# Wider moving operands in a hybrid token-mixer trunk: 512 weight columns past stationary activations

## The chip, the core and the metric

One NeuronCore of a Trainium2 chip. The metric is the device time of one execution in microseconds, the median of several runs.

## The reference, cut to what matters

Two layers over 256 tokens and a model width of 1024, all in float32. `h` is a layer norm, modulated by adaLN; `w_in` has 14248 columns, which go to four token mixers, their gates `z` and the merge gates.

```python
for l in range(2):
    shift, scale, gate = split(silu(c) @ w_ada[l] + b_ada[l], 3)
    h = layernorm(x) * (1 + scale) + shift
    q_a,k_a,v_a, q_b,k_b,v_b,beta,decay, cq,ckv,kpe, qkv_d, z, merge = split(h @ w_in[l])
    o_a = diff_attention(...)        # branch A
    o_b = gated_delta_rule(...)      # branch B: short convolution, scan over 4 chunks of 64 tokens
    o_c = mla(...)                   # branch C
    o_d = dilated_attention(...)     # branch D: 3 dilations, 8 heads
    branches = stack([o_a, o_b, o_c, o_d]) * silu(z)
    merged = einsum('snc,ncd,snd->sd', branches, w_br[l], sigmoid(merge))
    x = layernorm(ALPHA * x + gate * (merged @ w_out[l])) * ln_g[l] + ln_b[l]
```

## The kernel before

**Split products.** A large product is made of three float32r matmuls for each 128 rows of the contraction. Each operand is split into a high part that float32r holds exactly and a low part: `hh` and `hl` for the activations, `wh` and `wl` for the weights. `load_w` (L519) fetches half a unit's weights as a tile of 128 x 1024 (512 KB) into `wr` on SP's DMA queue, ScalarE casts it to `wh` (L466), and VectorE (GpSimd for a few) subtracts to get `wl` (L470, L469). There are four buffers each of `wr`, `wh` and `wl`.

**Units.** `w_in` is cut into units of 256 columns (`UW`). A unit is 48 matmuls of 256 moving columns: 8 tiles of the contraction, 3 products, and 2 tiles of its output. Two forms exist:

- `token_proj` / `token_mm` (L546, L556), for the first four units, A and D: 128 tokens of `h^T` are stationary, 256 weight columns move. Both token tiles of a unit share one PSUM bank. For each of the two token tiles all eight contraction tiles are gone through.
- `feat_proj` (L564), for B, the gates `z`, the merge gates and the branch products (24 matmuls there): 128 weight columns are stationary, 256 tokens move, and features come out on the partitions.

The output projection (`do_out`, L1342) uses `token_mm` on `mh` and `ml`, the merged values with features on partitions.

**PSUM.** Eight banks: three for these products ("mm"), two for branch B, two for scores, one for transposes. Queries and keys of A and D go through `rotated_transpose` (L576): ScalarE copies the unit (L581), VectorE rotates part of it (L424 to L427), and the transposes `tu_...` (L588) are kept back until the matmuls of one more unit are issued (`deferred`, `flush`).

**The order of work.** `layer_items` makes a list of items, one for each unit and each quarter of a branch product: first units, B (6), rest of A (4), then the phases of the branches C, A, B, D in that order. A phase is 2 gate units, and 4 times a merge unit and a quarter of the branch product. Half of D's units stands between the phases of C and A, the other half between A and B. Weights are fetched two items ahead (`AHEAD`). The mixers are generators; after each item `step_streams` moves each running one on by a rate (`RATE`: B, A, D 1.0; C 2.0; adaLN of the next layer 0.7 steps). A phase's first gate unit (`do_z`, u = 0) first runs what is left of its branch at once (`finish`). The order on each engine is then made by a list scheduler from this program order and its own simulated times.

**Written orders.** In the first layer the adaLN sums are made from loaded weights, and the first units are multiplied by quarters of the contraction as `h^T` comes; four matmuls with a zero operand open their banks, and `start_order` (L438) fixes the order on the engines. Before the second layer, `in_order` puts the power of the layer norm (`pow`, on GpSimd) between the subtractions of weight pieces.

Of the kernel before, what the change touches and what calls it, by code (L numbers as in the profile page):

```python
# [15 lines left out]
ALU = mybir.AluOpType  # L16
# [16 lines left out]
UW = 256  # L33
SLABS = {"b": 20, "q": 14, "c": 4, "d": 6, "tk": 2, "hf": 4, "p": 8, "o": 6}
# [3 lines left out]
HT1 = 3  # L38
# [6 lines left out]
START_VECTOR = ((0, 0), (1, 0), (1, 1), (3, 1))  # L45


def _unit_columns():
    """Column ranges of w_in in units of up to 256, and whether a unit's weights are stationary."""
    units, where = [], {}  # L50

    def add(name, start, n, feat):
        where[name] = len(units)
        for u in range(0, n, UW):
            units.append((start + u, min(UW, n - u), feat))
# [9 lines left out]
    return units, where  # L65


UNITS, WHERE = _unit_columns()
# [71 lines left out]
def _layout(a):  # L140
# [10 lines left out]
    wi = np.zeros((L, len(UNITS), 2, P, 1024), f32)  # L151
    for u, (c0, n, feat) in enumerate(UNITS):
        cols = np.zeros((L, 8, P, UW), f32)
        cols[..., :n] = w_in[..., c0:c0 + n]
        if u == WHERE["ckv"]:
            cols[..., n:n + 8] = w_in[..., OFF["beta"]:OFF["beta"] + 8]
        if feat:
            wi[:, u] = cols.reshape(L, 8, P, 2, P).transpose(0, 3, 2, 1, 4).reshape(L, 2, P, 1024)
        else:
            wi[:, u] = cols.reshape(L, 2, 4, P, UW).transpose(0, 1, 3, 2, 4).reshape(L, 2, P, 1024)  # L160
    out["win"] = wi
    w = a["w_br"].reshape(L, 4, 4, P, 4, UW)
    out["wbr"] = np.ascontiguousarray(w.transpose(0, 1, 4, 3, 2, 5)).reshape(L, 4, 4, P, 1024)
    w = a["w_out"].reshape(L, 2, 4, P, 4, UW)
    out["wout"] = np.ascontiguousarray(w.transpose(0, 4, 1, 3, 2, 5)).reshape(L, 4, 2, P, 1024)
# [31 lines left out]
def kernel(ctx: ExitStack, tc: tile.TileContext, d, out, dbg=None, nlayers=DEPTH):  # L197
# [34 lines left out]
    # ------------------------------------------------------------ first loads  # L232
# [31 lines left out]
    zero = cpool.tile([P, P], BF16, name="zero")  # L264
    G.memset(zero, 0.0)
# [10 lines left out]
    # ------------------------------------------------------------ silu(c), adaLN  # L276
# [69 lines left out]
    # ------------------------------------------------------------ constants of the mixers  # L346
# [70 lines left out]
    # ------------------------------------------------------------ helpers  # L417
    def rope(dst, src, nh, n, name):
        """dst, src: [P, 2, nh, 2 * n]; src may be in PSUM."""
        cc, ss = rt[n]  # L420
        tmp = s2.tile([P, 2, nh, 2 * n], F32, tag="ropet", name=f"ropet_{name}")
        ccb = cc.rearrange("p t a n -> p t (a n)").unsqueeze(2).to_broadcast([P, 2, nh, 2 * n])
        ssb = ss.rearrange("p t a n -> p t (a n)").unsqueeze(2).to_broadcast([P, 2, nh, 2 * n])
        V.tensor_tensor(tmp[:, :, :, 0:n], src[:, :, :, n:2 * n], ssb[:, :, :, 0:n], ALU.mult)  # L424
        V.tensor_tensor(tmp[:, :, :, n:2 * n], src[:, :, :, 0:n], ssb[:, :, :, n:2 * n], ALU.mult)
# [11 lines left out]

    def start_order():  # L438
        """The order of issue in the first layer's first units, engine by engine."""
        m = marks  # L440
        in_order(m["his00"], m["mod00"], m["h00"], m["his10"], m["his20"], m["his30"])
        in_order(m["acc0"][7], m["los00"], m["hl00"], m["los10"])
        in_order(m["acc2"][4], m["hl01"], m["acc2"][5])
        in_order(m["acc3"][7], m["hl03"])
        in_order(m["q0"][35], m["sum01"], m["q0"][36])
        in_order(m["q1"][23], m["sum02"], m["q1"][24])
# [18 lines left out]
    def split(hi, lo, src, eng=V):  # L465
        marks["hi"] = A.copy(hi, src)  # L466
        if eng is G:
            parts = (tuple(v[:, j:j + 512] for v in (lo, src, hi)) for j in range(0, src.shape[-1], 512))
# [3 lines left out]
    def softmax(dst, ssum, sc, mask, name):  # L472
        """dst = exp(sc + mask - max) and its row sums; sc in PSUM, dst in SBUF."""
# [5 lines left out]
    def pair_scores(lhs, rhs, t, tag, name, nb):  # L479
        """exp of causally masked scores of two maps [P, 2, n], unnormalised, and reciprocal sums [P, 2]."""  # L480
# [15 lines left out]
    def causal_transpose(prs, m, tag, name):  # L496
        """P^T of one map as [P keys, 3, P]: (keys 0, queries 0), (0, 1), (1, 1)."""
# [7 lines left out]
    # ------------------------------------------------------------ projections  # L505
    deferred = []

    def flush():
        """Emits what waits for the matrix products of one more unit."""
        while deferred:  # L510
            deferred.pop(0)()
# [7 lines left out]
    def load_w(src, name, place=None, eng=V):  # L519
        """Half a unit's weights; a function giving columns of the parts that float32r holds exactly."""  # L520
        w = wraw.tile([P, 1024], F32, tag="wr", name=f"wr{name}")
        nc.sync.dma_start(w, src)
# [4 lines left out]
        else:  # L527
            width = 512
# [3 lines left out]
        for j, (a, b) in enumerate(zip(hi, lo)):  # L532
            marks[f"lo{name}"] += split(a, b, w[:, j * width:(j + 1) * width], eng)
            marks[f"hi{name}"].append(marks["hi"])

        def get(c0, n):
            return tuple(a[c0 // width][:, c0 % width:c0 % width + n] for a in (hi, lo))
# [3 lines left out]
    def spare():  # L541
        """Slabs of the attention branches for two more units' weights."""
# [13 lines left out]
    def token_proj(w, hh, hl, name, sel=natural):  # L556
        """[P tokens, 2, 256] in PSUM = h @ w for both token tiles; w: two halves of four d tiles."""
        ps = bank("mm", [P, 2, UW], name)
        for t in range(2):
# [888 lines left out]
```

## Time and profile before

| | us |
|---|---|
| runs: median (lowest to highest of 3) | 1084.03 (1082.26 to 1086.2) |
| span of the profiled execution, first to last instruction | 1080.6 |
| TensorE matmul busy | 1046.7 (97%) |
| TensorE weight load busy | 1003.7 (93%) |
| VectorE busy | 749.0 (69%) |
| ScalarE busy | 557.3 (52%) |
| GpSimd busy | 68.7 (6%) |

The profiled execution has no time of its own beside its span; its 1080.6 us stand 3.4 us below the median of the runs, for what lies around the program's first and last instruction and for the spread of the runs. A matmul's busy time contains the way through the array and overlaps with its neighbours, so the distance between starts, or a count over a stretch, tells the pace, and the mean duration does not.

### The profile page before, as it was taken

To read this page: it belongs to the slowest core of one execution; us is meant where nothing else is said; L and a number is where in the kernel's file an instruction comes from. 1 tells how busy PE (TensorE), PEld (TensorE's weight loads), DVE (VectorE), ACT (ScalarE), POOL (GpSimd) and SP (SyncE) were. 2 spreads that over 40 slices of the span, in tenths; PEclk is the share of its full clock that TensorE was granted. 3 is DMA by queue.
4 is the path that set the end of the run, shared out by engine and by line. 5 is a ranking of instruction groups with operands and counts; after the bars stand their busy time and mean duration, and the time that the engine had idled before them with its cause. 6 is when DMAs were issued, how large, how long until landed. Compare 5 with 4: busy or idle time off the path is not lost. (4 is left out here: it accounts for less than half of the span.)

```text
span 1080.6 us, 21300 instructions
## 1 busy us (share of the span) xinstructions
PE 1046.7 (97%) x8490; PEld 1003.7 (93%) x8490; DVE 749.0 (69%) x1576; ACT 557.3 (52%) x1018; POOL 68.7 (6%) x62
## 2 busy tenths in 40 slices
PE   4799999999999999999989999999999999999997
PEld 3799999999999999999979999899999999999997
DVE  6888778786576664567894886778656555565776
ACT  4376675555454354546535666655455444454550
POOL 2300000010000000000450000001000000000000
PEclk9899999999999999999989999999999999999999
DMA  9963334557554565347762333446644236533551
GB/s 322 326 234 119 118 117 169 182 209 244 169 181 144 192 239 174 118 156 228 228 237 64 135 135 119 160 171 201 194 159 138 98 118 234 178 135 124 199 185 40
DMA packets 67812, 186.24 MB, mean 172 GB/s; under 512 B 13569, under 2 KB 20097, under 8 KB 67713
## 3 DMA queue, kind: packets, MB, share of 16 engines
q1 hardware_dynamic: 67712, 184.88, 49.8%
q8 instruction: 67, 1.10, 0.4%
q14 instruction: 33, 0.26, 0.1%
HBM read 180.39 MB, written 4.46 MB: 171 GB/s over the span
## 5 line engine op out<-in xcount | busy, mean ns | idle before, releaser
L470 DVE TENSOR_TENSOR wl<-wr,wh 128x1024 fp32r<-128x1024 f32 x248 | 303.6, 1226 | 175.2 <-ACT wh L466 174.2
L466 ACT CAST wh<-wr 128x1024 fp32r<-128x1024 f32 x252 | 264.0, 1048 | 279.4 <-PE d L552 99.9
L551 PE MATMUL d<-wh,hh 128*128 128x256 f32 x576 | 166.1, 288 | 0.0
L553 PE MATMUL d<-wl,hh 128*128 128x256 f32 x576 | 163.8, 284 | 0.0
L552 PE MATMUL d<-wh,hl 128*128 128x256 f32 x576 | 163.6, 284 | 0.0
L570 PE MATMUL m<-hh,wh 128*128 128x256 f32 x512 | 148.0, 289 | 0.0
L572 PE MATMUL m<-hh,wl 128*128 128x256 f32 x512 | 146.3, 286 | 0.0
L571 PE MATMUL m<-hl,wh 128*128 128x256 f32 x512 | 145.6, 284 | 0.0
L551 PEld LDWEIGHTS d<-wh,hh 128*128 128x128 f32 x576 | 110.9, 193 | 0.6 <-issue 0.6
L553 PEld LDWEIGHTS d<-wl,hh 128*128 128x128 f32 x576 | 110.8, 192 | 0.5 <-issue 0.5
L552 PEld LDWEIGHTS d<-wh,hl 128*128 128x128 f32 x576 | 110.9, 192 | 0.2 <-issue 0.2
L570 PEld LDWEIGHTS m<-hh,wh 128*128 128x128 f32 x512 | 97.5, 190 | 2.6 <-issue 1.4
L571 PEld LDWEIGHTS m<-hl,wh 128*128 128x128 f32 x512 | 97.6, 191 | 0.8 <-issue 0.6
L572 PEld LDWEIGHTS m<-hh,wl 128*128 128x128 f32 x512 | 97.5, 190 | 0.8 <-issue 0.5
L302 DVE SCALAR_TENSOR_TENSOR ada<-wada,cact,ada 128x512 f32<-128x512 f32 x84 | 68.1, 816 | 20.9 <-DMA wada<-in_wada 19.9
L570 PE MATMUL z<-hh,wh 128*128 128x256 f32 x256 | 73.9, 289 | 0.0
L570 PE MATMUL br<-bh,wh 128*128 128x256 f32 x256 | 73.8, 288 | 0.0
L572 PE MATMUL z<-hh,wl 128*128 128x256 f32 x256 | 72.8, 284 | 0.0
L571 PE MATMUL z<-hl,wh 128*128 128x256 f32 x256 | 72.7, 284 | 0.0
L571 PE MATMUL br<-bl,wh 128*128 128x256 f32 x256 | 72.5, 283 | 0.0
L572 PE MATMUL br<-bh,wl 128*128 128x256 f32 x256 | 72.0, 281 | 0.0
L570 PE MATMUL b<-hh,wh 128*128 128x256 f32 x192 | 56.2, 293 | 0.0
(366 smaller groups left out, 2467.7 us busy)
## 6 DMA issues: line engine op xcount, KB each, us to landing
wr<-in_win SPq DMA_DIRECT2D x212, 512.0 KB
wr<-in_wbr SPq DMA_DIRECT2D x32, 512.0 KB
wada<-in_wada SPq DMA_DIRECT2D x32, 512.0 KB
wada<-in_wada SPq DMA_DIRECT2D x32, 256.0 KB
wrs<-in_win SPq DMA_DIRECT2D x8, 512.0 KB
wro<-in_wout SPq DMA_DIRECT2D x8, 512.0 KB
wr<-in_wout SPq DMA_DIRECT2D x8, 512.0 KB
wrearly<-in_win SPq DMA_DIRECT2D x4, 512.0 KB
```

Source lines behind the costliest of these rows:

```text
L302: return V.scalar_tensor_tensor(acc, w, cd, acc, ALU.mult, ALU.add)
L466: marks["hi"] = A.copy(hi, src)
L470: return [V.tensor_tensor(lo, src, hi.bitcast(F32), ALU.subtract)]
L551: ins.append(T.matmul(ps, a, wh, start=(k == first), stop=False))
L552: ins.append(T.matmul(ps, b, wh, start=False, stop=False))
L553: ins.append(T.matmul(ps, a, wl, start=False, stop=(k == last)))
L570: T.matmul(ps[:, f, :], wh, hh(k), start=(k == 0), stop=False)
L571: T.matmul(ps[:, f, :], wh, hl(k), start=False, stop=False)
L572: T.matmul(ps[:, f, :], wl, hh(k), start=False, stop=(k == nk - 1))
```

## The change

Where activations can be stationary, 512 weight columns move instead of 256. Units of A and D are paired to 512 columns; merge gates, branch products and the output projection, too, have tokens stationary and 512 columns moving. The first units become one of 424 columns (latents and beta, decay) and one of 512. B and the gates `z` keep `feat_proj`. A 512 column unit has four pieces of two contraction tiles, and each token tile has a PSUM bank of its own. The merged values then have tokens on partitions, and `merged_T` transposes them ahead of the output projection. D's nine units for four heads are four of 512 columns, and one more holds a value part of all eight heads. The orders written by hand at the start and before the second layer are gone, the rates of the generators are as before.

```diff
-    add("ckv", OFF["ckv"], 160, False)
-    add("b", OFF["qb"], 1536, True)
-    add("cq", OFF["cq"], 256, False)
-    add("a", OFF["qa"], 1536, False)
-    add("d", OFF["qkvd"], 4608, False)
+    add("first", [(OFF["cq"], 416), (OFF["beta"], 8)])
+    for i in range(3):
+        add("a", [(OFF["qa"] + TW * i, TW)])
+    for i in range(6):
+        add("b", [(OFF["qb"] + UW * i, UW)], True)
+    add("dv", [d_(2, 0, 0), d_(2, 0, 1)])
+    for hv in range(2):
+        for pair in DPAIRS:
+            add(f"d{hv}", [d_(s, g, hv) for s, g in pair])
     for n in range(4):
-        add(f"z{n}", OFF["z"] + 512 * n, 512, True)
-        add(f"m{n}", OFF["merge"] + 1024 * n, 1024, True)
+        for i in range(2):
+            add(f"z{n}", [(OFF["z"] + 512 * n + UW * i, UW)], True)
+        for i in range(2):
+            add(f"m{n}", [(OFF["merge"] + 1024 * n + TW * i, TW)])
...
-    def token_mm(ps, w, ah, al_, t, ks, first, last):
+    def token_mm(ps, w, ah, al_, t, p, first=False, last=False):
+        n = ps.shape[-1]
         ins = []
-        for k in ks:
-            wh, wl = w[k // 4]((k % 4) * UW, UW)
+        for i in range(2):
+            k = 2 * p + i
+            wh, wl = w[p](i * n, n)
             a, b = ah(k, t), al_(k, t)
-            ins.append(T.matmul(ps, a, wh, start=(k == first), stop=False))
-            ins.append(T.matmul(ps, b, wh, start=False, stop=False))
-            ins.append(T.matmul(ps, a, wl, start=False, stop=(k == last)))
+            ins.append(T.matmul(ps, a, wh, start=(first and i == 0), stop=False))
+            ins.append(T.matmul(ps, a, wl, start=False, stop=False))
+            ins.append(T.matmul(ps, b, wh, start=False, stop=(last and i == 1)))
         return ins
...
+    SKEW = {4: ((0, 0), (1, 0), (0, 1), (2, 0), (1, 1), (3, 0), (2, 1), (3, 1)),
+            2: ((0, 0), (1, 0), (0, 1), (1, 1))}
+
+    def token_unit(w, ah, al_, name, done):
+        np_ = len(w)
+        ps = [None, None]
+        for p, t in SKEW[np_]:
+            if p == 0:
+                ps[t] = bank("mm", [P, TW], f"{name}{t}")
+            token_mm(ps[t], w, ah, al_, t, p, p == 0, p == np_ - 1)
+            if (p, t) == (1, 0):
+                flush()
+            if p == np_ - 1:
+                done(t, ps[t])
+                if t == 1:
+                    flush_but_last()
...
-        A.copy(tv[:, :, :, 16:64], pv[:, :, :, 16:64])
-        rope(tv[:, :, :, 0:16], pv[:, :, :, 0:16], 4, 8, name)
+        A.copy(tk[:, :, 16:64], pv[:, :, 16:64])
+        rope(tk[:, :, 0:16], pv[:, :, 0:16], 8, 8, name, t)
...
-            pt = bank("mm", [P, 2, S], f"tu_{name}")
-            for pr in range(2):
-                for t in range(2):
-                    T.transpose(pt[:, pr, t * P:(t + 1) * P], tk[:, t, pr * P:(pr + 1) * P], ident)
+            pt = bank("mm", [P, 4, P], f"tu_{name}")
+            for pr in range(4):
+                T.transpose(pt[:, pr, :], tf[:, pr * P:(pr + 1) * P], ident)
+            for j, (dst, scale) in enumerate(zip(dsts, scales)):
+                o, i = dst[:, :, t * P:(t + 1) * P], pt[:, 2 * j:2 * j + 2, :]
...
-                for p_ in (a.rearrange("p t (b n) -> p (t b) n", n=P) for a in ps):
-                    T.matmul(p_, zero, zero.unsqueeze(1).to_broadcast([P, 4, P]), start=True, stop=False)
...
                 first_ada(0)
-                for i in range(4):
-                    load_half(i, 0)
+                for i in range(2):
+                    load_piece(i, 0)
                 h_part([0, 1], [0, 1])
                 first_ada(1)
+                for i in range(2):
+                    load_piece(i, 1)
...
-                start_order()
...
             def do_br(u):
...
                     if last:
...
-                        A.mul(L.mh[u], L.acc[u], 0.25)
-                        V.scalar_tensor_tensor(fl(L.ml[u]), fl(L.acc[u]), 0.25, fl(L.mh[u].bitcast(F32)),
-                                               ALU.mult, ALU.subtract)
+                        deferred.append(lambda: merged_T(u, t))
...
+            def merged_T(u, t):
+                pt = bank("mm", [P, 4, P], f"mT{u}{t}_{l}")
+                for j in range(4):
+                    T.transpose(pt[:, j, :], L.acc[u, t][:, j * P:(j + 1) * P], ident)
+                for j in range(2):
+                    i, ts = 2 * u + j, slice(t * P, (t + 1) * P)
+                    src = pt[:, 2 * j:2 * j + 2, :]
+                    A.mul(L.mh[i][:, :, ts], src, 0.25)
+                    V.scalar_tensor_tensor(L.ml[i][:, :, ts], src, 0.25, L.mh[i][:, :, ts].bitcast(F32),
+                                           ALU.mult, ALU.subtract)
 
             for u in range(2):
                 add(units(f"z{n}", u), do_z(u))
-            for u in range(4):
+            for u in range(2):
                 add(units(f"m{n}", u), do_m(u))
...
-                order = [(u, range(8)) for u in range(4)]
-                if t == 0:
-                    order = [(u, range(6)) for u in range(3)] + [(u, (6, 7)) for u in range(3)] + [(3, range(8))]
+                order = [(0, (0, 1)), (1, (0, 1)), (0, (2, 3)), (1, (2, 3))] if t == 0 else [(0, range(4)), (1, range(4))]
...
-            if i + 1 in starts and i > 0:
-                nm = f"a{starts.index(i + 1)}0"
-                pieces = [marks[f"lo{i + 1}_{j}"] for j in range(4)]
-                in_order(pieces[0], pieces[1], marks[f"pow{nm}"], pieces[2], pieces[3])
```

## Rows read from the trace of the kernel before

**Rows 1.** The page, head and part 1: busy us, share, instructions.
```profile
span 1080.6 us, 21300 instructions
...
PE 1046.7 (97%) x8490; PEld 1003.7 (93%) x8490; DVE 749.0 (69%) x1576; ACT 557.3 (52%) x1018; POOL 68.7 (6%) x62
```

**Rows 2.** Waits of TensorE, whole execution: us in total, times, longest.
```profile
PE hT L660 <- ACT xn L463: 12.7, 3, 8.8
PE adac L310 <- DVE ada L302: 6.6, 2, 4.7
```

**Rows 3.** Windows: us, busy and instructions by engine, clock, DMA share, GB/s.
```profile
core 0: us, PE busy (x) PEld busy (x) DVE busy (x) ACT busy (x) POOL busy (x), PEclk, DMA share, GB/s
0.00:61.50 61.50, 40.37 (x247) 36.24 (x248) 47.12 (x98) 28.29 (x67) 16.99 (x19) 0.94 0.85 306
34.90:37.30 2.40, 2.40 (x12) 2.40 (x13) 0.42 (x1) 2.23 (x8) 0.00 (x0) 0.50 1.03 397
...
483.50:529.40 45.90, 45.90 (x387) 45.90 (x386) 34.62 (x41) 28.01 (x37) 0.60 (x1) 1.00 0.70 230
```

**Rows 4.** Timeline of TensorE at the half clock: start us, us, instruction.
```profile
35.44 0.41 PE L553 MATMUL first<-wls,hh 128*128 128x256 f32 x1
35.65 0.41 PE L551 MATMUL first<-whs,hh 128*128 128x256 f32 x1
```

**Rows 5.** Timeline: float32 matmuls in a row, start us, us of all.
```profile
65.24 0.96 PE L788 MATMUL psel<-ckv,cf 128*128 128x8 f32 x8
...
75.37 1.46 PE L1085 MATMUL pq<-wuq,cqT 128*128 128x192 f32 x8
...
108.41 1.88 PE L1113 MATMUL pvc<-wukv,ckT 128*128 128x512 f32 x4
```

**Rows 6.** Groups by line and form: count, busy us, mean ns of one.
```profile
L588 PE MATMUL tu_d<-cf,tkd 128*128 128x128 f32 x96 | 14.4, 272 | 0.0
L1085 PE MATMUL pq<-wuq,cqT 128*128 128x192 f32 x64 | 11.4, 326 | 0.0
L1113 PE MATMUL pvc<-wukv,ckT 128*128 128x512 f32 x8 | 3.8, 592 | 0.0
L788 PE MATMUL psel<-ckv,cf 128*128 128x8 f32 x16 | 2.0, 241 | 0.0
```

**Rows 7.** Groups by line: one of three products each of D, merge, branch.
```profile
L551 PE MATMUL d<-wh,hh 128*128 128x256 f32 x576 | 166.1, 288 | 0.0
...
L570 PE MATMUL m<-hh,wh 128*128 128x256 f32 x512 | 148.0, 289 | 0.0
...
L570 PE MATMUL br<-bh,wh 128*128 128x256 f32 x256 | 73.8, 288 | 0.0
```

**Rows 8.** Timeline: one D unit's copy, rotation and transposes.
```profile
384.38 0.47 ACT L581 COPY tkd<-d 128x384 f32<-128x384 f32 x1
...
387.06 0.29 DVE L427 TENSOR_TENSOR tkd<-tkd,ropet_d 128x128 f32<-128x128 f32 x1
...
389.54 0.60 PE L588 MATMUL tu_d<-cf,tkd 128*128 128x128 f32 x4
```

**Rows 9.** Timeline of VectorE behind the last matmul.
```profile
1072.77 0.42 DVE L1374 TENSOR_TENSOR gy<-y,gateb 128x256 f32<-128x256 f32 x1 [1.53 <-PE y L553]
...
1074.14 0.26 DVE L453 BATCH_NORM_AGGREGATE bnmvp<-bnstp 128x2 f32<-128x24 f32 x1
```

**Rows 10.** Groups by line: subtraction and cast of a weight piece.
```profile
L470 DVE TENSOR_TENSOR wl<-wr,wh 128x1024 fp32r<-128x1024 f32 x248 | 303.6, 1226 | 175.2 <-ACT wh L466 174.2
L466 ACT CAST wh<-wr 128x1024 fp32r<-128x1024 f32 x252 | 264.0, 1048 | 279.4 <-PE d L552 99.9
```

**Rows 11.** Groups by line and form: branch B's scan, both layers.
```profile
L1025 PE MATMUL pS<-vn,g_ktil 64*128 64x128 f32 x48 | 7.1, 298 | 0.0
L993 PE MATMUL pv<-g_vb,g_U 128*128 128x128 f32 x32 | 6.5, 296 | 0.0
L1006 PE MATMUL po<-vn,g_Q 128*128 128x128 f32 x32 | 6.4, 293 | 0.0
...
L1032 DVE SCALAR_TENSOR_TENSOR S<-S,egl,pS 128x128 f32<-128x128 f32 x16 | 4.7, 343 | 1.6 <-PE pS L1025 1.6
```

More of the change, by code (lines that the diff above doesn't have):

```diff
@@ L263 @@
     G.memset(ones, 1.0)
-    zero = cpool.tile([P, P], BF16, name="zero")
-    G.memset(zero, 0.0)
     marks = {}
@@ L415, in load_constants, with rope @@
             V.tensor_scalar(subs[:, l:l + 1], smc("subln", l), 1.0 - li, None, ALU.mult)
[L418 to L425, printed above, removed]
+    def rope(dst, src, nh, n, name, t=None):
+        cc, ss = (a.rearrange("p t a n -> p t (a n)") for a in rt[n])
+        shape = [P, 2, nh, 2 * n] if t is None else [P, nh, 2 * n]
+        tmp = s2.tile(shape, F32, tag="ropet", name=f"ropet_{name}")
+        ccb, ssb = ((a.unsqueeze(2) if t is None else a[:, t].unsqueeze(1)).to_broadcast(shape) for a in (cc, ss))
+        V.tensor_tensor(tmp[..., 0:n], src[..., n:2 * n], ssb[..., 0:n], ALU.mult)
+        V.tensor_tensor(tmp[..., n:2 * n], src[..., 0:n], ssb[..., n:2 * n], ALU.mult)
         V.tensor_tensor(dst, src, ccb, ALU.mult)
@@ L467, in split @@
         if eng is G:
-            parts = (tuple(v[:, j:j + 512] for v in (lo, src, hi)) for j in range(0, src.shape[-1], 512))
+            parts = (tuple(v[:, j:min(j + 512, v.shape[-1])] for v in (lo, src, hi)) for j in range(0, src.shape[-1], 512))
             return [G.tensor_tensor(a, b, c.bitcast(F32), ALU.subtract) for a, b, c in parts]
@@ L631, with pieces, first_pieces @@
         pass
-    def first_halves(l):
-        return [d["win"][l, WHERE[n] + i, h] for n, i in (("ckv", 0), ("cq", 0), ("a", 0), ("a", 1)) for h in range(2)]
+    def pieces(l, name, i=0):
+        u = WHERE[name][i]
+        n = 1024 if UNITS[u][1] else 2 * sum(n for _, n in UNITS[u][0])
+        return [d["win"][l, q, :, 0:n] for q in PIECES[u]]
+    def first_pieces(l):
+        return pieces(l, "first") + pieces(l, "a", 0)
     def layer_items(l, prev):
@@ L641, in units @@
         def units(name, i=0):
-            return [d["win"][l, WHERE[name] + i, h] for h in range(2)]
+            return pieces(l, name, i)
         def hh(k):
@@ L681, in layer_start, with first_bank @@
             L.hf = [slab("hf", [P, 2, S], f"hf{l}{i}") for i in range(4)]
-            names = [("ckv", 0), ("cq", 0), ("a", 0), ("a", 1)]
-            ps = [bank("mm" if i < 3 else "b", [P, 2, UW], f"first{i}_{l}") for i in range(4)]
+            n0 = 424
+            ps = [[None, None], [None, None]]
+            def first_bank(i, t):
+                ps[i][t] = bank("b" if (i, t) == (1, 1) else "mm", [P, (n0, TW)[i]], f"first{i}{t}_{l}")
             ah, al_ = lambda k, t: natural(L.hh, k, t), lambda k, t: natural(L.hl, k, t)
@@ L717, in layer_start @@
                 first_ada(2)
-                load_half(0, 1)
-                load_half(1, 1)
+                for i in range(2):
+                    load_piece(i, 2)
                 h_part([0, 1], [4, 5])
@@ L722, in layer_start @@
                 first_ada(3)
-                load_half(2, 1)
-                load_half(3, 1)
+                for i in range(2):
+                    load_piece(i, 3)
                 h_part([0, 1], [6, 7])
@@ L1135, in branch_c, with take_a, done, token_item @@
                 A.copy(L.oT[2][hp // 2][:, hp % 2, :], po)
-        L.qa, L.ka, L.va = [], [], []
-        def take_a(u, ps):
-            dst = slab("q", [P, 2, S], f"qkva{u}_{l}")
-            (L.qa, L.ka, L.va)[u // 2].append(dst)
-            if u < 4:
-                rotated_transpose(dst, ps, 0.125 if u < 2 else 1.0, f"a{u}_{l}")
-            else:
-                A.copy(dst, ps)
-            if u == 5:
-                L.sa = start("a", branch_a())
-        for u in range(2, 6):
-            add(units("a", u), lambda w, u=u: take_a(u, token_proj(w, L.hh, L.hl, f"a{u}_{l}")))
+        L.qkva = [None] * 3
+        def take_a(u):
+            dst = L.qkva[u] = [slab("q", [P, 2, S] if u < 2 else [P, TW], f"qkva{u}{j}_{l}") for j in range(2)]
+            def done(t, ps):
+                if u < 2:
+                    rotated_transpose(dst, (0.125 if u == 0 else 1.0,) * 2, ps, t, f"a{u}{t}_{l}")
+                else:
+                    A.copy(dst[t], ps)
+                    if t == 1:
+                        L.sa = start("a", branch_a())
+            return done
+        def token_item(name, sel, done):
+            return lambda w: token_unit(w, lambda k, t: sel(L.hh, k, t), lambda k, t: sel(L.hl, k, t), name, done())
+        for u in range(1, 3):
+            add(units("a", u), token_item(f"a{u}_{l}", natural, lambda u=u: take_a(u)))
         def branch_a():
@@ L1394, in do_out @@
                 in_order(marks["eps" + nm], *marks["gy01"], marks["nmr" + nm], *marks["gy11"], *marks["gy21"], marks["gy31"][0])
-        add([d["wout"][l, u, h] for u in range(2) for h in range(2)], do_out)
+        add([d["wout"][l, 0, p] for p in range(4)], do_out)
         return L
```

233 lines of the change are left out of this document (123 added, 110 removed).

## The prediction

> **What bounds the kernel now.** I read the page's first part, then the waits, then the stages, then single rows. The page has TensorE busy for 97% of a span of 1080.6 us [rows 1], but ends of matmuls are modelled there, so this alone says little. The waits decide: in the whole execution TensorE waited for other engines only 26 us in eight groups, the two largest 12.7 us for normalised activations (at the start and between the layers) and 6.6 us for the sums of the adaLN weights (at the start) [rows 2]. From 61.5 us on, but for the change of layer, each matmul waits for the matmul before it. VectorE is busy 69%, ScalarE 52% [rows 1]. So from the first unit on time is a count of matmuls times their pace; before 61.5 us DMA (306 GB/s), VectorE's adaLN sums and the half clock count as well.
>
> The pace: in 483.5 to 529.4 us the program runs only gate, merge and branch products, by the code 96 + 192 + 96 = 384 matmuls of 256 columns, in 45.9 us at granted clock 1.00 (2.4 GHz) [rows 3]: **119.5 ns each**. Is this streaming or something beside it? In 34.9 to 37.3 us the granted clock was 0.50 (1.2 GHz) [rows 3], and there the same shape starts every 0.21 us (35.44, then 35.65) [rows 4]: 256 columns in 213 ns is one column per cycle, with nothing added. At the full clock that would be 107 ns; the row has 119.5. The float32 matmuls show what else there is: with (whole stretch less one mean)/(count less one), 192 columns start every (1.46-0.326)/7 = 0.162 us, 512 every (1.88-0.592)/3 = 0.429, so 0.834 ns a column with some 2 ns on top; but 8 columns still take (0.96-0.241)/7 = 0.103 [rows 5, 6]. So a matmul costs the longer of its stream plus 2 ns and a floor, which I read as the load of 128 stationary columns: about 0.10 us for float32, 119.5 ns for this kernel's split weights, whose stream of 107 + 2 lies below it. A stream of 512 columns, 213 + 2 = **215 ns**, would lie above it.
>
> **The change, part by part.** *Fewer, wider matmuls.* The three products of a split (activation high and low by weight high and low) stay three; halved in number are, per layer, a, d, merge, branch, output and the first units: from 2592 matmuls (d alone has 3 x 576 in both layers, merge 3 x 512, branch 3 x 256 [rows 7]) to 1248 of 512 columns and 48 of 424. z and B stay. A pair saves 2 x 119.5 - 215 = 24.0 ns, one of 424 columns (177 + 2) saves 60. The first unit of layer 0 is set by loads and sums, so I give it nothing (if only its last two quarters count, 2 us). 1200 + 1248 pairs x 24.0 + 48 x 60 = **-61.6 us**. No row has 512 split columns at the full clock. Bounds: if 119.5 is a rate per column, 512 take 239 and nothing is saved; if the excess of 12.5 ns is a fixed price of every matmul, 226, saving -34.7; I take 215, since the half clock shows neither price nor slope beyond one column a cycle.
>
> The Trainium skill ("TensorE: Matmul & The Clock Gate", Back-to-back issue gap) gives N/2.4 + 2.5 ns, 109 at 256 columns and 216 at 512. By that rule at both widths a pair of 512 saves 2.5 ns and one of 424 some 39, 8 us instead of 61.6 in all; with the give-backs below the time would be 1100. The trace does not pay 109 at 256 but 119.5, so the measured number stands there; at 512 the rule and my line agree. The section's other figure, 131 ns a matmul of 512 columns in a stream, would need four columns a nanosecond where the half-clock rows give one a cycle; no run here shows it, and I give it no chance.
>
> *Merged values now come out with tokens on partitions*, so merged_T transposes them: 16 a layer at (0.60-0.272)/3 = 0.109 us [rows 6, 8], **+3.5 us** on TensorE, since it never waits there. Copies double in number at half the width, on ScalarE and VectorE, which have idle time there (28.0 and 34.6 of 45.9 us busy [rows 3]).
>
> *Output and change of layer.* Each 512 column bank now feeds two quarters of the post-norm. After the last matmul one set more of multiply, add and statistics follows, from 1072.77 to 1074.14 [rows 9]: **+1.4 us** at the end. Between the layers the same 1.4 us is added to both token tiles' chains, while their cover shrinks: the output products of the second tile from 96 x 119.5 = 11.5 to 48 x 215 = 10.3 us, and then the first unit's half. The order that put the power on GpSimd between weight pieces is dropped; a piece is some 1.4 us. I take **+6 us**, between 0 and 9.
>
> *PSUM banks.* A q or k unit used one of three banks for 48 x 119.5 = 5.7 us; now each token tile takes one, and its transposes another. The next unit's second tile needs a bank 2.6 us after the unit's end. Example: copy at 384.38, rope ends at 387.35, transposes at 389.54, so 3.0 us from copy to rope end, hidden in 5.7 [rows 8]. The first tile ends 2.6 us early, so its bank comes round at about the right time; one late rope in three stalls. 14 units at 0.4: **+6 us**; bounds 0 and 2 us each, 28.
>
> *Weight pieces.* All four buffers now belong to one unit. A piece's buffer comes free 4 or 5 of the 8 steps (each 6 x 215 = 1.3 us) before its successor is used: 5.2 us for a cast of 1.05 and a subtraction of 1.23 [rows 10] and their queues. 38 units at 0.1: **+3 us**; bounds 0 and 0.5 each, 19. DMA needs 0.5 MB per 2.6 us, 203 GB/s, against 306 seen [rows 3].
>
> *Branches step once per item*, and the items fall from 70 to 43 a layer. Counting yields: B has 36 steps and 43 items before its gate, afterwards 24, so its scan over chunks (12 steps) is run at once when z1 asks for it; C is 2 of 20 steps short at z2; A and D still finish. The scan's matmuls take some 15 us a layer (three groups of 7.1, 6.5 and 6.4 us in both layers [rows 11], two narrower ones of about 5 each), its state updates 2.4 [rows 11]; with copies and some 15 hops between engines I estimate 30 us. Its cover: z1 11.5, first merge unit 10.3, and its own 15 on TensorE, 37 in all. **+4 us**, between 0 and 50.
>
> *Start.* Loads are 0.27 MB fewer in another order, the zero matmuls and the written order go: 0, between -2 and +4; VectorE was busy 47.1 of 61.5 us there [rows 3].
>
> Sum: -61.6 + 3.5 + 1.4 + 6 + 6 + 3 + 4 = -37.7, so the span goes to 1042.9. The median of the runs lies 3.4 us above the profiled span (1084.0 to 1080.6); with that, **1046 us**.
>
> **Rivals.** *Fixed price per matmul:* 226 ns at 512; 34.7 instead of 61.6 saved gives 1073. For it: 119.5 is 12.5 above the stream. Against: 213 at the half clock, 2 ns in float32 rows.
>
> *Waits replace the pace:* banks and weight buffers at their upper bounds (47 instead of 9 us) give 1084, no change; halfway 1065. For it: ropes that end late, casts released directly by TensorE. Against: VectorE idle 31%.
>
> *Slower, streaming rate:* if reading float32 split operands is what limits 256 columns to 119.5, 512 take 239, only the narrow unit saves 2, give-backs stay: 1106. It decides from 230 ns a matmul on: there 24 us of give-backs eat the saving. Against: 0.834 ns a column in float32 needs half that rate, so no row excludes it; but a coincidence with one column a cycle at half clock is needed.
>
> *Slower, B's scan uncovered:* if other branches' work and missing weights leave z1 waiting, 30 us a layer, +56 over my sum: 1102; it decides from 21 us a layer on.
>
> **Chances.** Main case 0.60 (1046, own range 1028 to 1062), fixed price 0.12, waits 0.15 (0.08 faster, 0.04 same, 0.03 slower), rate 0.07, scan 0.06 (0.01 still faster). 0.3% of 1084, 3.3 us, is about what a measurement tells from no change: faster 0.81, same 0.04, slower 0.15. The range 1028 to 1084 leaves out 0.02 below and 0.15 above.
>
> **What would show it.** A merge or d stretch without other work must show 512 columns starting every 215 ns (226 or 239 for the rivals). Phase 3, with z and 16 transposes, should fall from 45.9 to 11.5 + 96 x 0.215 + 48 x 0.215 = 42.5 us plus transposes. Waits of TensorE for rope copies or for wl, absent now, would show banks and pieces; a gap before br1 the scan. Wrong makes me a pace above 230, or waits beyond 38 us.

## The result, and the profile after

The changed kernel takes **1101.9 us** (median of 4 runs, 1097.9 to 1103.5) against 1083.2 us before (4 runs now, 1082.3 to 1086.2): the ratio is **1.0166, 95% interval 1.0142 to 1.0189**. It is slower; 1046 us, faster, was forecast. The profiled execution has a span of 1100.1 us and took 1101.9.

The head of the page and its first part, for the changed kernel; it answers to [rows 1]:

```profile
span 1100.1 us, 16201 instructions
...
PE 1041.5 (95%) x5926; PEld 874.5 (79%) x5926; DVE 743.7 (68%) x1585; ACT 563.3 (51%) x1060; POOL 58.2 (5%) x61
```

TensorE has 2564 matmuls fewer and is busy 5 us less, yet the span is 19.5 us longer. Two things must be told apart: how fast wide matmuls go, and what else became longer.

**The pace.** Windows of the changed kernel, columns as in [rows 3]: a merge unit in the second layer with nothing beside it, then the merge phase of branch B in the first layer, then that of branch D.

```profile
1002.80:1013.70 10.90, 10.90 (x49) 9.01 (x48) 6.28 (x9) 4.81 (x5) 0.00 (x0) 1.00 0.48 146
402.90:488.30 85.40, 80.09 (x491) 65.22 (x490) 49.02 (x96) 35.61 (x65) 3.27 (x4) 0.94 0.42 134
488.30:533.40 45.10, 42.74 (x239) 36.76 (x239) 33.88 (x45) 24.37 (x38) 0.00 (x0) 1.00 0.72 240
```

By the code the first window holds the unit's 48 matmuls: 10.90/48 = **227 ns** each, not 215, at the full clock. In the timeline of branch B's last product in the first layer (start us, us, instruction) the starts lie 0.23 to 0.24 apart:

```profile
482.74 0.39 PE L556 MATMUL br<-wh,bh 128*128 128x512 f32 x1
482.97 0.40 PE L557 MATMUL br<-wl,bh 128*128 128x512 f32 x1
483.21 0.39 PE L558 MATMUL br<-wh,bl 128*128 128x512 f32 x1
```

Here it is 231 to 237 ns. The last window answers to the stretch of [rows 3] for which 42.5 us was forecast, from 45.9; it is 45.1, and a part of its branch products lies behind it.

**Where TensorE's time went.** I added up, for all matmul records, the time from each start to the next start on TensorE, by what is produced; waits ahead of the next matmul are thus in the row of the one before it. The sums are the spans. The third column is an experiment below (B's rate at 1.8).

| us, whole span | before | after | B's rate 1.8 |
|---|---|---|---|
| D units | 212.1 | 204.8 | 203.4 |
| merge gates | 191.0 | 183.2 | 183.4 |
| branch products | 94.9 | 94.7 | 93.9 |
| branch A's units behind the first ones | 49.3 | 45.8 | 45.8 |
| output product, with the gap behind it | 57.3 | 65.8 | 67.3 |
| merged_T | 0 | 5.0 | 4.8 |
| start, first units, hT, adaLN sums | 95.4 | 90.6 | 90.3 |
| z and b (not changed) | 166.4 | 167.2 | 168.5 |
| all other pieces, nearly all float32 pieces of the branches | 214.3 | 243.0 | 221.6 |
| sum | 1080.6 | 1100.1 | 1079.1 |

The widened rows gain 18.9 us (D 7.3, gates 7.8, branch products 0.2, branch A 3.5) where 2 x 119.5 - 215 promised three times that. The small pieces of the branches, whose number did not change, lose 28.7, the output product 8.5, the transposes 5.0.

**Waits.** TensorE's waits in the changed kernel (us in total, times, longest). The first answers to the first of [rows 2], whose longest lay at the start; the others have no row there:

```profile
PE hT L682 <- ACT xn L459: 9.5, 2, 8.5
...
PE br L556 <- DVE zth L1329: 3.2, 1, 3.2
...
PE m L556 <- ACT mg L1339: 1.9, 1, 1.9
...
PE mT L1367 <- DVE acc L1352: 1.7, 1, 1.7
PE mT L1367 <- ACT who L462: 1.2, 1, 1.2
```

The first is at the change of layer. Its timeline in the changed kernel, and under it the same place before:

```profile
563.41 0.40 PE L558 MATMUL y<-who,ml 128*128 128x512 f32 x1
572.35 0.97 PE L682 MATMUL hT<-cf,xn 128*128 128x128 f32 x3 [8.54 <-ACT xn L459]
```

```profile
552.21 0.28 PE L552 MATMUL y<-who,ml 128*128 128x256 f32 x1
555.56 1.18 PE L660 MATMUL hT<-cf,xn 128*128 128x128 f32 x4 [2.96 <-ACT xn L463]
```

The gap behind the output product grew from 3.0 to 8.5 us. The second wait is the one the scan rival named, ahead of branch B's first product in the first layer:

```profile
436.61 0.39 PE L558 MATMUL m<-wh,hl 128*128 128x512 f32 x1
...
461.17 0.44 PE L1014 MATMUL pot<-cf,on 128*128 128x128 f32 x2 [0.69 <-DVE on L1049]
464.76 0.79 PE L556 MATMUL br<-wh,bh 128*128 128x512 f32 x1 [3.16 <-DVE zth L1329]
465.35 0.63 PE L557 MATMUL br<-wl,bh 128*128 128x512 f32 x1
465.78 0.63 PE L558 MATMUL br<-wh,bl 128*128 128x512 f32 x1
466.21 0.63 PE L556 MATMUL br<-wh,bh 128*128 128x512 f32 x1
```

The first of these rows is the last gate matmul ahead of B's product. From there to B's product, 28 us later, TensorE has only the small pieces of B's scan, which wait in turn for copies and updates on VectorE, and those of branch D. It idles 5.3 us in this phase, its granted clock falls (mean 0.94 in the window of 85.4 us above) and is 0.50 still in the last three rows, and the phase, 60.5 us before, takes 85.4 in the first layer and 79.2 in the second.

### The profile page after: what moved, and what is told of

The parts are those of the page before. It is cut to its first block, busy times and chain, and to the rows that moved or that the text cites. A ratio compares the mean times of both kernels' runs of the same rounds, so it can differ in the third digit from the quotient of the medians.

```text
span 1100.1 us, 16201 instructions
## 1 busy us (share of the span) xinstructions
PE 1041.5 (95%) x5926; PEld 874.5 (79%) x5926; DVE 743.7 (68%) x1585; ACT 563.3 (51%) x1060; POOL 58.2 (5%) x61
## 4 chain that ended last, share of the span: by engine, by line
PE 85%; DVE 6%; DMA 4%; ACT 3%; issue 1%; SPq 0%; POOL 0%; DVEq 0%; ACTq 0%; POOLq 0%
PE d L556 5%; PE d L558 5%; PE d L557 5%; PE m L557 5%; PE m L556 4%; PE m L558 4%; PE z L585 3%; PE z L587 3%; PE z L586 3%; PE br L556 2%; PE br L558 2%; PE br L557 2%; PE b L585 2%; PE b L586 2%; PE b L587 2%; DMA wada<-in_wada 2%
## 5 line engine op out<-in xcount | busy, mean ns | idle before, releaser
L557 PE MATMUL m<-wl,hh 128*128 128x512 f32 x256 | 102.1, 399 | 0.5 <-DVE wl L466 0.5
L556 PE MATMUL m<-wh,hh 128*128 128x512 f32 x256 | 100.7, 397 | 1.9 <-ACT mg L1339 1.9
L556 PE MATMUL d<-wh,hh 128*128 128x512 f32 x256 | 102.2, 403 | 0.0
L557 PE MATMUL d<-wl,hh 128*128 128x512 f32 x256 | 101.1, 396 | 0.0
L558 PE MATMUL m<-wh,hl 128*128 128x512 f32 x256 | 101.0, 394 | 0.0
L558 PE MATMUL d<-wh,hl 128*128 128x512 f32 x256 | 100.5, 394 | 0.0
L556 PEld LDWEIGHTS m<-wh,hh 128*128 128x128 f32 x256 | 48.1, 188 | 12.5 <-ACT mg L1339 2.1
L558 PEld LDWEIGHTS d<-wh,hl 128*128 128x128 f32 x256 | 48.5, 190 | 10.9 <-issue 1.2
L557 PEld LDWEIGHTS d<-wl,hh 128*128 128x128 f32 x256 | 48.6, 190 | 9.4 <-DVE tkd L433 0.3
L556 PEld LDWEIGHTS d<-wh,hh 128*128 128x128 f32 x256 | 48.3, 190 | 9.6 <-issue 0.5
L587 PE MATMUL b<-hh,wl 128*128 128x256 f32 x192 | 54.8, 285 | 0.0
```

The lines of the kernel that those rows point to most:

```text
L556: ins.append(T.matmul(ps, a, wh, start=(first and i == 0), stop=False))
L557: ins.append(T.matmul(ps, a, wl, start=False, stop=False))
L558: ins.append(T.matmul(ps, b, wh, start=False, stop=(last and i == 1)))
L587: T.matmul(ps[:, f, :], wl, hh(k), start=False, stop=(k == nk - 1))
```

## The experiments

All times are medians; ratios are to the kernel before, run on the same chip.

**1. The price of a matmul by itself.** Runs of 48 matmuls with nothing beside them:

```python
for i in range(n):
    k = 0 if same else (i % 8) * P
    m = (i % 2) * (1024 - width)
    T.matmul(p, st[:, k:k + cols], mv[:, m:m + width], start=(i == 0), stop=(i == n - 1))
```

> Not the reference's computation: runs of 48 matmuls into one bank with nothing beside them, which name their form: float32r with 256, 384 and 512 moving columns, 512 with the same stationary tile each time, 512 and 256 with 64 stationary columns, bfloat16 256 and 512, float32 512 and 256; the input goes to the output. Theory 1 (a matmul takes its columns at the full clock and some 13 ns more, whatever its width): 120 at 256, 173 at 384, 226 at 512. Theory 2 (the price at 512 comes from the traffic of other engines around it): 215 to 217 at 512, 120 at 256. The same stationary tile, or one half as wide, makes no difference under theory 1; it lowers 256 if the weight load sets that pace.

Groups by form of this run (count, busy us, mean ns of one): r is float32r, r512same takes the same stationary tile each time, r512c and r256c have 64 stationary columns, b is bfloat16. The last row is from the same view with weight loads (PEld).

```profile
L35 PE MATMUL r512c<-mov,sta 128*64 128x512 f32 x48 | 11.2, 392 | 0.0
L35 PE MATMUL r<-mov,sta 128*128 128x512 f32 x48 | 11.1, 390 | 0.0
L35 PE MATMUL r512same<-mov,sta 128*128 128x512 f32 x48 | 11.0, 389 | 0.0
...
L35 PE MATMUL b<-mb,sb 128*128 128x512 bf16 x47 | 10.5, 379 | 0.1
L35 PE MATMUL r<-mov,sta 128*128 128x384 f32 x48 | 8.5, 334 | 0.0
L35 PE MATMUL r<-mov,sta 128*128 128x256 f32 x48 | 5.9, 283 | 0.0
L35 PE MATMUL r256c<-mov,sta 128*64 128x256 f32 x48 | 5.6, 276 | 0.0
L35 PE MATMUL b<-mb,sb 128*128 128x256 bf16 x48 | 5.4, 273 | 0.0
...
L35 PEld LDWEIGHTS r512same<-mov,sta 128*128 128x128 f32 x48 | 9.0, 188 | 1.9
```

(Busy less one mean)/47 is the time from start to start: float32r 120 ns at 256 columns, 174 at 384, 228 at 512 (most starts lie 226 or 227 apart); bfloat16 109 and 215 (one of its 48 records is missing). At 2.4 GHz the columns alone take 107, 160 and 213. So float32r pays **13 to 15 ns a matmul, whatever the width**, and bfloat16 2 ns. As the excess does not shrink from 256 to 512 columns, it is no load of weights that a longer stream would cover. The same stationary tile 48 times takes 226 at 512, but its load was made 48 times all the same (the last row), so this does not show what a matmul without a load costs. Half as many stationary columns take 113 at 256, 7 less, which theory 1 did not expect, and 230 at 512, no less. Theory 1's price holds, theory 2 (traffic around it) falls; what the 13 ns are stays open.

The Trainium skill ("TensorE: Matmul & The Clock Gate", Back-to-back issue gap) gives N/2.4 + 2.5 ns, 109 and 216. The bfloat16 rows agree with both figures; the float32r rows, 120 and 226, agree with neither, and it is these that this kernel pays.

**2. Narrow again, all else as changed.** Each wide matmul becomes two of 256 (the first and the last of a bank stay whole).

```diff
-            ins.append(T.matmul(ps, a, wh, start=(first and i == 0), stop=False))
...
+                for c in range(0, n, n if start or stop or n != TW else UW):
+                    e = n if start or stop or n != TW else c + UW
+                    ins.append(T.matmul(ps[:, c:e], st_, mv[:, c:e], start=start, stop=stop))
```

> The changed kernel with its order of work, banks and rates, but each 512-wide matmul issued as two of 256 columns with the same stationary tile (the first and the last of a bank stay at 512). Theory 1 (a 512-wide matmul starts every 226 to 227 ns, so wide matmuls do save some 12 ns on each pair, and the loss lies in what came with them): halves at 119.5 ns make 239 a pair, some 2300 pairs by 12 to 13 ns is 28 to 30 us, so 1102 becomes 1125 to 1135. Theory 2 (512 is no better in place than two of 256, the loss is the width itself, by banks and weight buffers held longer): 1095 to 1108.

1107.1 us, ratio 1.0225 (1.0208 to 1.0242): 5 us more than wide, below the forecast of theory 1 and in the span of theory 2. Two windows, a quiet merge unit in each layer:

```profile
471.40:482.90 11.50, 11.50 (x94) 11.33 (x93) 7.32 (x9) 4.80 (x5) 0.00 (x0) 1.00 0.74 245
1007.80:1019.30 11.50, 11.50 (x94) 11.32 (x93) 6.09 (x7) 4.79 (x5) 0.00 (x0) 1.00 0.47 162
```

There the price is as expected: 11.5 against 10.9 us for 44 pairs, 14 ns a pair. Added up as above, D units took 6.5 us more, gates 6.2, branch A 2.3, branch products 1.4, but the branches' small pieces, and the waits behind them, took 6 less, the row of the start 4 and merged_T 2. So the same was done without the stall at B's gate (its rate at 1.8, next experiment):

> The changed kernel with B's rate at 1.8 and each 512-wide matmul issued as two of 256 columns (first and last of a bank whole): the first experiment again without the stall at B's gate. Some 2250 matmuls more. Theory 1 (the probe's prices hold in place, 2 x 120 for 227): 28 us more than the 1080 with wide matmuls, less what the stalls at a switch or a wait already held, so 1098 to 1110. Theory 2 (in place width gains the 5 us that the first experiment showed): 1083 to 1088.

1094.3 us, ratio 1.0110 (1.0093 to 1.0127), 14.4 more than wide at that rate and between the two theories. D units lose 11.4 us for 792 pairs (14 ns each), a 2.4 for 176 (14), gates 6.3 for 704 (9), branch products and output nothing. These are 20 us; the row of the start (5 us) and merged_T (2 us) took less with halves, and why was not traced. So on these rows width is worth the probe's 13 ns in the projections, two thirds of it in the gates, nothing in the products. Theory 1's sum of 28 us was twice too large, theory 2's 5 too small.

**3. B's stream faster.**

```diff
-RATE = {"b": 1.0, "c": 2.0, "a": 1.0, "d": 1.0, "ada": 0.7}
+RATE = {"b": 1.8, "c": 2.0, "a": 1.0, "d": 1.0, "ada": 0.7}
```

> The changed kernel with the step rate of branch B's stream at 1.8 in place of 1.0, so that its 36 steps again spread over the items ahead of its gate. Theory 1 (the last steps of the scan, run at once in front of the gate, are what the kernel lost): the stretch of the last merge phase that waits for B falls from 85 and 79 us to about 60 to 68, and the time from 1102 to 1065 to 1085. Theory 2 (the scan costs the same wherever it runs): 1095 to 1105.

**1079.9 us**, ratio 0.9973 (0.9960 to 0.9987), 22 us less than the changed kernel. The windows of B's merge phase in both layers:

```profile
413.90:472.00 58.10, 58.10 (x345) 49.37 (x345) 41.35 (x70) 31.43 (x53) 0.00 (x0) 1.00 0.64 213
...
938.40:995.60 57.20, 57.20 (x337) 48.37 (x337) 35.24 (x60) 30.69 (x49) 0.00 (x0) 1.00 0.46 156
```

The idle 5 us and the fallen clock are gone, and the phase takes 58.1 and 57.2 instead of 85.4 and 79.2; the phases ahead of it take 11 and 12 us more, since the scan's pieces now run between their units. Up to the end of that phase the layers gain 16 and 10 us; some 3 us of it in each are lost again between there and the end of the output product. Theory 1 holds. Then at 1.4, and with the other streams raised as well:

> The changed kernel with B's rate at 1.4 in place of 1.0, for the shape of the curve between 1102 (1.0) and 1080 (1.8). Theory 1 (each step left over for the gate costs about the same, some 0.9 us a layer and step): 1088 to 1094, half way. Theory 2 (only the sequential scan of the last steps costs, the forms ahead of it don't): 1079 to 1084.

> The changed kernel with the step rates of all streams raised by the fall in the number of items (b 1.8, c 2.45, a 1.5, d 1.5, ada 1.25). Theory 1: not worse than with B's rate alone, 1060 to 1085; a few us more come from branch D's and A's last steps and the adaLN sums that no longer run in a row. Theory 2 (streams don't matter): 1095 to 1105.

At 1.4: 1079.9, ratio 0.9974 (0.9962 to 0.9986), as at 1.8. With 24 items ahead of the gate, 1.4 gives 33 of the 36 steps, 1.0 gives 24. With three steps left over B's phase is 3 us longer than at 1.8 in each layer (61.5 and 60.3), which other stretches give back; with twelve the whole is 22 us longer. The cost is no equal price of each step; the time lies in the span of theory 2. All rates raised: 1082.1, 0.9993 (0.9984 to 1.0003), no better; the other streams were no loss.

**4. The same stall in the kernel before, and its rate.**

```diff
-RATE = {"b": 1.0, "c": 2.0, "a": 1.0, "d": 1.0, "ada": 0.7}
+RATE = {"b": 0.56, "c": 2.0, "a": 1.0, "d": 1.0, "ada": 0.7}
```

> The kernel before with the rate of branch B's stream at 0.56 in place of 1.0, so that its steps stand to the items ahead of its gate as in the changed kernel, and the rest runs at once there. Theory 1: it loses what the changed kernel lost in these stretches, 15 to 25 us over two layers: 1083 becomes 1098 to 1108. Theory 2 (scan at once is covered by float32r work that the scheduler puts between): 1080 to 1088.

1091.4 us, ratio 1.0080 (1.0065 to 1.0095): 9 us lost, between both theories. The merge phase of B in the first layer of this run:

```profile
409.50:488.10 78.60, 76.86 (x629) 69.03 (x629) 43.85 (x83) 35.08 (x61) 2.78 (x4) 1.00 0.34 114
```

It is 18 us longer than before, as in theory 1, but idle only 1.7 us and at full clock, and some 13.5 us of it come back in the phases ahead, which hold less of B. So the same 12 steps cost 9 us there and 22 here; the idle time and the clock in the changed kernel's first layer explain a part of the difference, the rest was not parted.

Is the later versions' gain only a better rate? The kernel before with b at 1.3:

> The kernel before with B's rate at 1.3 in place of 1.0. If the rate alone made the later versions faster than the kernel before, this is faster too, 1072 to 1079. If B's 36 steps, done ahead of its gate at 1.0, were no stall in the kernel before, it stays at 1080 to 1086.

1093.1 us, ratio 1.0092 (1.0073 to 1.0110), slower, which neither side expected. By the table's sums D's units take 7.2 us more and z and b 2. TensorE's timeline in a D unit of that run shows a wait of its transposes for the rotation, which is queued on VectorE behind B's forms:

```profile
231.05 0.28 PE L553 MATMUL d<-wl,hh 128*128 128x256 f32 x1
233.71 1.09 PE L588 MATMUL tu_d<-cf,tkd 128*128 128x128 f32 x4 [2.38 <-DVE tkd L427]
```

It is the only such wait of that run, so most of the 10 us is not explained by it. What the three rates of the kernel before show is that 1.0 fitted its 70 items a layer; for 43 items it does not.

**5. One part of the change alone.** First the projections and the output product wide, gates and branch products as before (256, features on partitions, no merged_T), B at 1.3 for the 59 items that this leaves (its expectation says 55):

```diff
-            add(f"m{n}", [(OFF["merge"] + 1024 * n + TW * i, TW)])
+            add(f"m{n}", [(OFF["merge"] + 1024 * n + UW * i, UW)], True)
...
-                        deferred.append(lambda: merged_T(u, t))
...
+                        A.mul(L.mh[u], L.acc[u], 0.25)
```

> The changed kernel with its wide projections and wide output product, but merge gates and branch products again as in the kernel before (stationary weights, 256 wide, features on partitions, no merged_T), and branch B's rate at 1.3 for the 55 items that this leaves. Theory 1 (a pair of 256 takes 239 ns and a 512 in place 230; the change of layer is longer because merged_T and the cover of the token chain changed): 1152 pairs give back 7 to 14 us, merged_T's 5 us and 5 to 8 us of the change of layer come back: 1070 to 1084. Theory 2 (the merge phases are where width pays, the projections' edits where it costs): 1085 to 1095.

**1077.3 us**, ratio 0.9949 (0.9933 to 0.9966), in the span of theory 1. Windows from z3 to the end of the last merge phase, and from there to B's first unit of the next layer:

```profile
483.80:530.50 46.70, 46.16 (x387) 45.95 (x385) 34.58 (x41) 27.92 (x37) 0.67 (x1) 1.00 0.69 222
530.50:584.90 54.40, 48.00 (x219) 39.77 (x217) 40.20 (x83) 26.55 (x55) 24.57 (x21) 0.94 0.53 175
```

Together 101.1 us. The same stretch, in the kernel before and in the changed one:

```profile
483.50:587.60 104.10, 99.18 (x793) 97.42 (x791) 75.72 (x120) 53.99 (x90) 27.03 (x21) 0.95 0.56 186
```

```profile
488.30:600.70 112.40, 98.36 (x489) 82.63 (x489) 83.10 (x142) 55.94 (x104) 24.02 (x21) 0.94 0.63 214
```

So with wide output and first units alone the stretch gains 3 us; with wide gates and products too, and merged_T in front of the output, it loses 8. The gap ahead of hT is 5.0 us here (8.5 in the changed kernel). Against the changed kernel with B's rate at 1.8 the rows of the table give 8.7 us more for gates and 5.4 for branch products, 8.9 less for the output, and merged_T's 4.8 are gone: there, wide gates and products gain about what they cost.

The other way round, the gates, products and output wide, D's and a's matmuls halved, b at 1.8:

> The changed kernel with B's rate at 1.8 and each matmul of a D unit and of branch A's second and third unit issued as two of 256 (first and last of a bank whole); gates, branch products, first units and output product stay wide. Theory 1: some 900 pairs by 8 to 13 ns are 7 to 12 us more than with B's rate alone: 1087 to 1092. Theory 2 (width in the projections gains nothing in place): 1078 to 1083.

1093.5 us, ratio 1.0090 (1.0067 to 1.0113), 13.6 more than with B's rate alone. In the profiled execution, the fastest of the four (1089.0), D units take 10.9 and a 2.4 more, and other rows 5 less. Width in the projections gains, as in theory 1, and 1.5 us more than its span.

**6. The transposes earlier.** b at 1.8, three merge phases wide; their sum is transposed ahead of the last phase, which is narrow with features on partitions.

```diff
-                    if last:
...
-                        deferred.append(lambda: merged_T(u, t))
+                    if n == 1 and t == 1:
+                        deferred.append(lambda: acc_T(u))
```

> The changed kernel with B's rate at 1.8, and the last merge phase of each layer alone (branch D's) again 256 wide with features on partitions: the sum of the other three is transposed in front of it, so that no transpose stands between the last branch product and the output product. Theory 1 (width gains some 8 to 13 ns a pair in the other three phases, and costs in the last one, because merged_T, the gates' Tanh and the later accumulation stand on the way to the output): the 60.5 and 69 us that the stretches from the last phase's first z to the end of the output product take in the kernel before come back from 79 and 74 to about 69 each, 5 to 12 us in all; 1066 to 1074. Theory 2 (the place of the transposes doesn't matter): 1078 to 1084.

**1074.7 us**, ratio **0.9937** (0.9918 to 0.9956), the fastest version here. Of the stretches named, z3 to the end of the output product, 79 and 74 us at that rate became 76 and 73, not 69 (before, both are 69; the 60.5 of the expectation is B's phase); the output row falls by 8.8 us to 58.5, but the transposes still cost 6.5, and z3 now waits for banks that they hold (waits of TensorE):

```profile
PE z L589 <- ACT accf L1375: 2.9, 2, 1.4
```

The time is near what theory 1 gave, its two stretches are not. The edit moves the transposes and narrows the last phase at once; what each is worth was not parted. With b at 1.4:

> As the mixed kernel, with B's rate at 1.4. Theory 1 (the stall at B's gate grows with the steps left over): at 1.4 about 34 of 36 steps are done ahead of the gate or nearly so, 0 to 8 us more than at 1.8. Theory 2 (any rate over 1.0 serves alike): within 2 us of it.

1079.7 us, ratio 0.9976 (0.9965 to 0.9988), 5 us more, as theory 1 had it. In the changed kernel 1.4 and 1.8 were alike; so the rate has no single best value across these versions.

**7. Does other traffic slow wide matmuls?** Branch and output products run mostly at 231 to 238 ns, not 227.

> Not the reference's computation: runs of 48 float32r matmuls of 512 columns with a new stationary tile each, one after the other: alone (quiet), with VectorE on SBUF, with VectorE reading PSUM, with ScalarE reading PSUM, with both, with 4 MB of loads, and two of 256 columns. Theory 1 (other engines' accesses add 4 to 10 ns to a wide matmul): 226 to 227 in the quiet ones, 230 to 237 with one or several of the others, 120 and up to 125 at 256. Theory 2 (the extra is the kernel's own order of operands or banks): 226 to 227 in all.

Groups of this run: the quiet one, VectorE on SBUF, VectorE reading PSUM, ScalarE reading PSUM:

```profile
L40 PE MATMUL quiet<-mov,sta 128*128 128x512 f32 x48 | 11.0, 389 | 0.0
L40 PE MATMUL vector<-mov,sta 128*128 128x512 f32 x48 | 11.0, 389 | 0.0
...
L40 PE MATMUL vecpsum<-mov,sta 128*128 128x512 f32 x48 | 11.0, 389 | 0.0
...
L40 PE MATMUL actpsum<-mov,sta 128*128 128x512 f32 x48 | 11.0, 389 | 0.0
```

The other engines' work fills these runs: 13 of VectorE's 14 instructions take 10.2 us of the 11, ScalarE's 16 take 11.5. All runs are at (11.0 - 0.389)/47 = 226 ns. For these, theory 1 falls. The loads had nothing to wait for and ran under the first run, not under the one that bears their name, and ScalarE and VectorE did not read at the same time; for loads the changed kernel's records answer: the wide matmuls without a break behind them start every 229.9 ns where the DMA engines were idle (some 700 of them) and every 230.3 where they were over 95% busy (some 600). So theory 1 falls for loads too.

What the records do show is a settling. Counted from the last break (a wait, or a float32 piece), the first four gate matmuls of 512 columns take 232.6 ns in the mean, the next four about 229, then about 228, and from the thirteenth on about 227. The probe of experiment 1 shows the like: behind its run of 384 columns the first nine of 512 start 225 to 236 apart, then 226 or 227. Branch products take 233 wherever they stand; before, at 256, they started every 117.7 in the mean, so that two took 235 and there was little for width to save. Why the break is felt so long, and why branch products never settle, stays open; over all wide matmuls the excess over 226.5 is 8 us.

## Why the prediction was wrong

**The step that failed first** is the reading of the pace: "a matmul costs the longer of its stream plus 2 ns and a floor", by which 512 columns would take 215 ns. The excess of 12.5 ns at 256 is a price beside the stream, paid at every width (experiment 1). The prediction had this as its *fixed price* rival at 226 and gave it 0.12. The half clock misled it: at 1.2 GHz no excess shows at 256. It was taken as proof that there is no price beside the stream, but it only shows that there is none at that clock. The rows of 512 columns at the half clock, shown under the waits, do the same in the changed kernel: 0.43 us from start to start, and 512 columns at 1.2 GHz are 0.427. The float32 rows misled it as well: their 2 ns is not float32r's 13. By count and price the whole change saves 36 us on TensorE's matmuls instead of 61.6 (6528 of 256 columns at 119.5 before; after, 1344 at 119.5, 96 of 424 at 191 and 2496 at 226.5; counts and paces from the records). The rate rival, 239, falls.

**In place even that was not reached.** The widened rows of the table gain 18.9 us, start, first units and sums 4.8. In the first units of layer 0 nothing was to be had, as predicted: B's first unit starts at 61.1 us, before at 61.5. Of the 12 us that are left, 8 is the excess of experiment 7, about 3 of it in branch and output products and the rest mostly behind breaks.

**"Branches step once per item"** was right as a mechanism (24 of 36 steps, the scan run at once at z1) and mis-sized: +4 us was taken, 22 measured (experiment 3). The cover of 37 us counted TensorE's own pieces and z1; in the trace the scan's matmuls stand from 402 to 461 us, 59 and not 30, z and the merge unit are through at 437, and the traces show TensorE idle 5.3 us and at a mean clock of 0.94 in that phase of the first layer. The rival's 30 us a layer was too much, since the phases ahead got back a part; 11 a layer is half of the 21 from which it was to decide alone. It decided together with the fixed price. That its sum, 1102, lies next to 1101.9 is luck: it keeps the pace of 215 and takes 30 us a layer, and the runs show neither.

**Output and change of layer**: +6, +1.4 and +3.5 for merged_T were predicted. merged_T takes 5.0, the output row with the gap behind it 8.5 more. That TensorE "never waits there" did not hold: merged_T waits for the sum and for ScalarE (2.9 us in the rows of waits), and it stands between the last branch product and the output. In the table the two are 13.5 together, against 10.9 predicted, and experiment 5 shows that they come from the wide gates and products and not from the wide output product: with the first narrow and the second wide, the output row is 58.4, before 57.3.

**Banks (+6) and weight pieces (+3)** were too dear: the waits have 1.9 us for a bank that a gate's Tanh holds (m <- mg) and 0.5 for wl in the whole execution. The waits for the rotation are 0.4 us, and VectorE's spare third was enough. That rival falls.

**The sum with measured terms**, on spans: widened rows -18.9, start and first units -4.8, small pieces of the branches +28.7 (21.4 of it B's stall, by the column at 1.8), output +8.5, merged_T +5.0, z and b +0.8: +19.3, where 1100.1 - 1080.6 = 19.5 was measured. The 7 us of small pieces that are left at b 1.8 were not traced to one cause.

## What to carry to other kernels

Measure the price of a matmul of the very type and width by itself before widening: an excess over the stream may be a floor, which width buys off, or a fixed price, of which width saves one for each matmul left out. Where background streams are stepped once per work item, fewer and larger items starve them; after a change of the items' size, count the steps done at each gate and set the rates anew. A layout that needs a transpose can cost more than its matmuls where it stands between a sum and the product that waits for it: here 5.0 us of transposes came with 8.5 us of longer output. In the middle of the work, beside a narrow last phase, the transposes took 6.5 us and the output was as before.

## What the runs showed of the hardware that was not expected

- float32r matmuls take columns/2.4 ns and 13 ns each at full clock (120, 174, 226 ns at 256, 384, 512 columns), bfloat16 ones 2 ns (109, 215), with as many stationary columns.
- Loading the same stationary tile again each time is no faster than loading a new one (226 at 512), and 64 stationary columns instead of 128 save 7 ns at 256 (113) and nothing at 512 (230).
- VectorE on SBUF or PSUM and ScalarE on PSUM beside them change nothing (226), nor do loads (229.9 and 230.3 in the kernel).
- Behind a break, the gates' wide matmuls need about a dozen to come down from 233 to 227 ns; in the probe, behind another width, it took nine.
- The first large matmul behind a wait or behind the branches' small float32 pieces takes some 80 to 110 ns more until the next start, at either width (mostly 310 to 340 at 512 in the changed kernel, 200 to 220 at 256 before); width saves none of that.
